# A two-layer decoder trunk: another timetable for the RWKV scan, with the Gram mask on GpSimd and the keys by per-channel constants

## The chip, the core and the metric

The kernel runs on one core of one Trainium2 chip. The metric is device time in microseconds (us) of one execution. The engines are TensorE (PE; its weight loads are shown as PEld), VectorE (DVE), ScalarE (ACT), GpSimd (POOL) and SyncE (SP, which only issues DMAs here). Each engine works through its own queue in order, and engines wait for each other by semaphores.

## The reference, cut to what matters

x is 512 x 2048 in float32. Layer 0 is gated differential attention, layer 1 is gated RWKV-7 time mixing. Each is `x + W_out(mixer(RMSNorm(x)) * silu(gate))`. All weights are float32. The second layer is:

```python
p = h @ w_in                                  # 2048 -> r, k, v, g of 2048 each, and two low ranks of 96
p = p + (token_shift(p) - p) * mu
decay = exp(-exp(w_log));  a = sigmoid(a0 + da @ iclr_up)
kk = k * k_k, normalised per head;  k = k * (1 + (a - 1) * k_a)
# per head (32 heads of 64), over 512 tokens:
sa = S @ (-kk_t);  S = S * w_t + sa (kk_t * a_t)' + v_t k_t';  y_t = S @ r_t
y = groupnorm(y) + sum(r * k * r_k) * v
out = x + (y * silu(g)) @ w_out
```

## The kernel before, in words

**Products.** Every float32 product with a weight is made of three float32r matmuls (`mm3`, L108): high times high, high times low, low times high. The weights arrive by DMA on SP (`load_w`, L78); ACT writes the high part (`split_w`, L96) and DVE the low part (L97), in two buffers each, so the split of one group can begin when PE is through with the group two before it. One group is 24 matmuls of 512 columns. These matmuls to the PSUM tile `pp` are called filler below, because the small work of the scan is laid between them.

**Layer 1** goes through 16 pairs of heads (`layer1`, loop over j). A round has four projections of 48 matmuls each: k, r and v of pair j and, from j = 3 (`LAG`), the gate of pair j-3. Beside them run:

- `stage1`: decay and learning rate; the cumulative sum of the log decay (`tensor_tensor_scan`, L731), its exponentials `E` and `l`; the tile `BK`, which holds for each head both the b vector and the key, each times `l` (L748, L751, L753, all on DVE); `AR` (a and r times `E`).
- `gram` (called after 15 of v's 48 matmuls, argument `behind`): BK' AR per chunk of 64 tokens into PSUM `gp` (L781), masked by the constant `gmask` on DVE into `p.G` (L788). The blocks that make a triangular system go out to DRAM (`ltd`, DMAs on POOL, L795 and L801) and come back as `LT` (L825).
- `t_solve`: 31 steps of two DVE instructions (L836, L838) on `LT` give `Tm`, which goes out as `td` (SP, L840).
- a chain of steps for the pair before (`chain`, `Chain`): `t_combine` loads `TT` (L852), transposes a part (`T1`, L860, DVE) and completes it with two sets of small matmuls, `px` (L866, L876). `scan_pair` then goes over 8 chunks. Each chunk has three small matmuls, each followed by a hand-over: `sm` L943, copied to `rhs` on ACT (L946); L954, copied to `VS` on ACT (L956); L961, from which DVE makes the next state in `VS` (L965, for the first chunk L968). POOL copies the state (`SA`, L949) and scales it (`Sg`, L952); L965 reads `Sg`, and the ACT copy L956 overwrites what L949 reads.
- `outputs` (PSUM `Y`, L983, L987), `centre`, `group_norm`, `finish_y` and, three rounds later, `gate`.

**What orders it.** `tick` counts filler matmuls. When a chain's count (`gap` after the two ACT hand-overs, `gap_s` after the state) is used up, its next step may be issued after that matmul (`issue_after`); a scheduler then places it in each engine's queue by a modelled time and a priority, of which the scan's (`SCAN`) stands over that of the weights (`AHEAD`). `Chain.held` adds a condition: a step that needs ACT or DVE (`taker`) waits while the position `at` in the projection lies in certain windows. In rounds 3 to 14 the gaps are 5 and 5 matmuls, else 4 and 4, and in the last chain 3 and 4.

**Between the layers** (`layer0`, L554 to L569) the row norms of the new x are needed before the first matmul of layer 1: sums of squares (`ssx`), `rsqrt` as a row of small DVE operations for three row tiles, then for the fourth, and x scaled by it (L566).

Of the kernel before, what the change touches and what calls it, by code (L numbers as in the profile page):

```python
# [23 lines left out]
P = 128  # L24
# [80 lines left out]

def mm3(nc, out, aH, aL, bH, bL, start, stop, g=None, at=0):
    for i, (a, b, s, e) in enumerate(((aH, bH, start, False), (aH, bL, False, False), (aL, bH, False, stop))):
        m = nc.tensor.matmul(out, a, b, start=s, stop=e)  # L108
        if g:
            tick(g, m, at + i)  # L110
    return m


class Chain:

    def __init__(self, g, steps, delay=0):
        self.steps, self.wait, self.taker = steps, delay, None  # L120
        g.chains.append(self)

    def step(self, g):
        with g.tc.high_priority(offset=SCAN):
            self.wait, self.taker = next(self.steps, (None, None))
        if self.wait is None:
            g.chains.remove(self)
# [12 lines left out]
def tick(g, m, at):  # L140
# [179 lines left out]
def attention(g, h, qkT, qkL, sq, V, VL, G, gap, rows=None):  # L320
# [64 lines left out]
    for i in range(NT + 3):  # L385
        if 0 < i <= NT:
            turn(i - 1)
        if i > 2:
            turn_y(i - 3)
        if i == NT + 2:  # L390
            break
        yield 8, None
        if 1 < i < NT + 2:
            weigh(i - 2)
        if i < NT:
            scores(i)
        yield gap - 8, None
    if rows is None:
# [34 lines left out]
def layer0(g, aps):  # L433
# [71 lines left out]
    with ExitStack() as cx:  # L505
# [3 lines left out]
        for h in range(NH):  # L509
# [5 lines left out]
            def keys(t1s=t1s, qkT=qkT):  # L515
                for t in range(NT):
                    turn_qk(g, t1s, *qkT, t)
                    yield 20, None

# [31 lines left out]

        rs = g.small.tile([P, NT], F32, name="rs1", tag="rs1", bufs=1)
        ss = g.small.tile([P, NT], F32, name="ss1", tag="ss1", bufs=1)
        for a, b in ((0, NT - 1), (NT - 1, NT)):  # L554
            nc.vector.reduce_sum(ss[:, a:b], g.ssx[:, a:b, :], AX.X)
            nc.vector.tensor_scalar(ss[:, a:b], ss[:, a:b], 1.0 / D, EPS, ALU.mult, ALU.add)
            rsqrt(g, rs[:, a:b], ss[:, a:b], b - a, f"r{b - a}")

        def more_h(n, m):
            for k in range(len(g.hH), min(n, KT)):  # L560
                xq, c0 = xs[k // 4], k % 4 * P
                ps = g.ps.tile([P, 512], F32, name="xT", tag="pa", bufs=2)
                for t in range(NT):
                    if c0 == 0:
                        with tc.high_priority(offset=AHEAD):
                            nc.vector.tensor_scalar(xq[:, t, :], xq[:, t, :], rs[:, t : t + 1], None, ALU.mult)  # L566
                    with tc.issue_after(m.ins) if m else ExitStack():
                        nc.tensor.transpose(ps[:, t * P : (t + 1) * P], xq[:, t, c0 : c0 + P], g.ident[:])
                with tc.high_priority(offset=AHEAD):  # L569
                    make_h(g, ps, KT + k)  # L570
# [33 lines left out]
def unit_chan(g, parts, cols, step=P, more=None, behind=(0, None)):  # L604
# [6 lines left out]
    for k0 in range(0, KT, KG):  # L611
        wh, wl = split_w(g, parts, KG, cols, k0)
        for k, c in [(k, c) for k in range(KG) for c in range(n)]:
            s = slice(c * step, (c + 1) * step)
            kk = k0 + k
            if more and c == 0:
                more(kk + 2, m)
            m = mm3(nc, pts[c][:step, :], wh[:, k, s], wl[:, k, s], g.hH[kk][:], g.hL[kk][:],
                    kk == 0, kk == KT - 1, g, 3 * kk)
            if n == 1 and 3 * kk + 3 == behind[0]:  # L620
# [14 lines left out]
C = 64  # L635
# [8 lines left out]
def rwkv_consts(g, aps):  # L644
# [17 lines left out]
    for nm, i, a, b in (("hw0", 0, 0.5, 0.0), ("ha0", 1, 0.5, 0.0), ("kk", 2, 1.0, 0.0), ("nkk", 2, -1.0, 0.0),  # L662
# [4 lines left out]
        g.prm[nm] = o  # L667


def rwkv_masks(g):  # L670
# [3 lines left out]
    nc.gpsimd.memset(g.rmask[:, :, 0:1], 0.0)  # L674
    g.TT = c.tile([P, NC_, 2, C], F32, name="TT")
    nc.gpsimd.memset(g.TT[:], 0.0)
    g.gmask = c.tile([P, P], BF16, name="gmask")
    nc.gpsimd.memset(g.gmask[:], 1.0)
    for lo in (0, C):
        r = slice(lo, lo + C)  # L680
        nc.gpsimd.affine_select(out=g.gmask[r, 0:C], in_=g.gmask[r, 0:C], compare_op=ALU.is_ge, fill=0.0,
                                base=-1, pattern=[[1, C]], channel_multiplier=-1)
        nc.gpsimd.affine_select(out=g.gmask[r, C:P], in_=g.gmask[r, C:P], compare_op=ALU.is_ge, fill=0.0,
                                base=0, pattern=[[1, C]], channel_multiplier=-1)
    g.hdec = c.tile([P, 1], F32, name="hdec")
# [28 lines left out]
def stage1(g, j, k, up):  # L714
# [32 lines left out]
    nc.scalar.activation(f[:], tha[:], AF.Identity, bias=col("omka"), scale=col("hka"))  # L747
    nc.vector.scalar_tensor_tensor(tha[:], tha[:], 1.0, k[:], ALU.add, ALU.mult)  # L748
    nc.vector.tensor_mul(f[:], f[:], k[:])
    for h, r_ in ((0, slice(0, C)), (1, slice(C, P))):  # L750
        nc.vector.scalar_tensor_tensor(BK[r_, :, h, :], ch(tha[r_, :]), col("hkk")[r_, :], l[r_, :, :],  # L751
                                       ALU.mult, ALU.mult)
        nc.vector.tensor_mul(BK[r_, :, 1 - h, :], ch(f[r_, :]), l[r_, :, :])  # L753
    k2 = w.tile([P, T], F32, name="k2", tag="thg", bufs=1)
# [15 lines left out]
def gram(g, j, p, before):  # L770
# [15 lines left out]
    for c0, gp in halves:  # L786
        for h in range(2):
            nc.vector.tensor_mul(p.G[:, c0 : c0 + 4, :, h, :], gp[h][:].rearrange("p (u x t) -> p u x t", u=4, x=2),  # L788
                                 g.gmask[:].rearrange("p (x t) -> p x t", x=2)[:, None].to_broadcast([P, 4, 2, C]))
    ps = g.ps.tile([P, 512], F32, name="pt", tag="pb", bufs=2)  # L790
# [55 lines left out]
def t_combine(g, j, p):  # L846

    nc, w, TT = g.nc, g.work, g.TT
    for h in range(2):
# [8 lines left out]
    for h in range(2):  # L858
        r_ = slice(h * C, h * C + C)
        nc.vector.transpose(T1[r_], TT[r_, :, h, 0:HALF])  # L860
    yield GAP_D, None
    N = NC_ * HALF
# [7 lines left out]
    for h, b0, _, _ in blocks:  # L870
        r_ = slice(b0, b0 + C)
        nc.scalar.copy(p.G[r_, :, 0, h, :], p.AR[r_, :, 0, :])
    yield GAP_X, None
    for h, b0, lo, hi in blocks:
# [3 lines left out]
    for h, b0, lo, _ in blocks:  # L878
        nc.scalar.copy(TT[lo, :, h, HALF:C], px[lo, N:].rearrange("p (c s) -> p c s", c=NC_))
    yield GAP_T, "ACT"  # L880

# [50 lines left out]
def scan_pair(g, j, p, gap, gap_s, others):  # L932
# [8 lines left out]
    for c in range(NC_):  # L941
# [8 lines left out]
        if 0 < c < NC_ - 1:  # L950
            Sg = w.tile([P, C], F32, name="Sg", tag="Sg", bufs=2)
            nc.gpsimd.tensor_scalar(Sg[:], p.SA[:, c - 1, :], p.gam[:, c : c + 1], None, ALU.mult)  # L952
        yield gap, "ACT"
        nc.tensor.matmul(sm[:, P : P + C], both(g.TT[:, c]), rhs[:], start=True, stop=True)  # L954
        for h, r_ in HEADS:
            nc.scalar.copy(VS[r_, c, h, :], sm[r_, P : P + C])  # L956
        yield (gap, "DVE") if c < NC_ - 1 else (gap, None)
        if c == NC_ - 1:
# [10 lines left out]
        if c in others:  # L969
            others[c]()  # L970
        yield gap_s, "ACT"
    outputs(g, j, p)
# [53 lines left out]
def layer1(g, aps):  # L1026
    nc, tc = g.nc, g.tc
    with ExitStack() as cx:
# [6 lines left out]
        for j in range(D // P):  # L1035
# [29 lines left out]

            vps = proj(2, behind=(15, behind))
            stage_v(g, j, p, vps)
# [11 lines left out]
        gps = [proj(3, i) for i in (j - 1, j)]  # L1079
        rows = split_rows(g, g.yd2, ("r", "k"), 2, j - 1)  # L1080
        rows.append(gate(g, j - 1, pairs[j - 1], gps[0], True))
# [4 lines left out]
        for cb in range(4):  # L1086
            cs = slice(cb * 512, (cb + 1) * 512)
            pts = unit_tok(g, yH, yL, [(aps["rw_w_out"][0], cb * 512, 512)], 512, 2)
            for t in range(NT):
                xr = w.tile([P, 512], F32, name="xr1", tag="rk"[t % 2], bufs=2)  # L1090
                nc.sync.dma_start(out=xr[:], in_=g.xd[t * P : (t + 1) * P, cs])
# [49 lines left out]
```

## Time and profile before

| what | us |
|---|---|
| runs before: median of 3 (lowest to highest) | 2263.07 (2261.76 to 2263.41) |
| profiled execution | 2254.08 |
| its span, first to last instruction | 2252.3 |
| PE busy in it | 2178.0 (97%) |
| DVE busy | 1422.2 (63%) |
| ACT busy | 955.2 (42%) |
| POOL busy | 228.8 (10%) |

A row of the grouped view gives line, engine, operation, tiles (output <- inputs), shape and count, then busy time and mean ns of one, then the idle time of the engine just ahead of them with what ended it. A row of the timeline gives start, duration, engine, line, tiles and, in brackets, the idle time ahead of it and its releaser. A row of the waits reads: waiting engine and line <- releaser: us in total, number of times, longest. Matmuls overlap in the pipeline and their ends are modelled: a 512-column matmul is shown with 0.39 us, while the next one starts 0.23 us after it.

### The profile page before, as it was taken

The numbers are of one execution on the slowest core, as the hardware profiler recorded it, in microseconds if no ns is written. First come the engines' busy times: TensorE is split into PE (matmuls) and PEld (weight loads), VectorE is DVE, ScalarE is ACT, GpSimd is POOL, SyncE is SP. The second block draws the span as 40 slices with busy tenths as digits, with TensorE's granted clock in tenths as the row PEclk, the third lists the DMA queues.
The fourth block names the chain that finished last, engine by engine and source line by source line (L and its number), as shares of the span: only waits on it lengthen the run. The fifth ranks groups of instructions, "written<-read, shape, count | busy, mean of one in ns | idle before, by whom it ended". The sixth has DMA issues, their size and how long they took to land. (4 is left out here: it accounts for less than half of the span.)

```text
span 2252.3 us, 33774 instructions
## 1 busy us (share of the span) xinstructions
PE 2178.0 (97%) x12260; PEld 1770.4 (79%) x12260; DVE 1422.2 (63%) x3783; ACT 955.2 (42%) x1969; POOL 228.8 (10%) x612
## 2 busy tenths in 40 slices
PE   8999999999999999989999999999999999999999
PEld 6888888888888878867767777777777777777887
DVE  5555646465564673346778887777777888776322
ACT  5443434344343452224355545545454455545211
POOL 0000000000000000000222212222222222222000
PEclk9999999999999999989999999999999999999999
DMA  6222232222322263323423233333333333334433
GB/s 179 93 86 95 84 100 88 93 94 82 97 85 94 94 214 108 136 77 87 105 66 77 78 87 95 87 90 89 85 89 80 89 88 90 96 97 127 140 131 112
DMA packets 290729, 224.45 MB, mean 100 GB/s; under 512 B 47732, under 2 KB 255748, under 8 KB 290564
## 3 DMA queue, kind: packets, MB, share of 16 engines
q1 hardware_dynamic: 275892, 195.74, 29.3%
q0 software_dynamic: 6144, 10.84, 2.0%
q10 hardware_dynamic: 8528, 15.73, 1.8%
q8 instruction: 96, 1.57, 0.3%
q14 instruction: 69, 0.57, 0.1%
HBM read 202.26 MB, written 19.99 MB: 99 GB/s over the span
## 5 line engine op out<-in xcount | busy, mean ns | idle before, releaser
L97 DVE TENSOR_TENSOR wl<-wraw,wh 128x1024 fp32r<-128x1024 f32 (+2 forms) x325 | 396.0, 1219 | 541.2 <-ACT wh L96 534.6
L96 ACT CAST wh<-wraw 128x1024 fp32r<-128x1024 f32 (+2 forms) x325 | 339.9, 1046 | 595.0 <-PE pp L108 404.1
L108 PE MATMUL pp<-wh,hH 128*128 128x512 f32 x1408 | 554.4, 394 | 6.0 <-ACT hH L588 5.7
L108 PE MATMUL pp<-wh,hL 128*128 128x512 f32 x1408 | 552.3, 393 | 0.0
L108 PE MATMUL pp<-wl,hH 128*128 128x512 f32 x1408 | 552.2, 392 | 0.0
L108 PE MATMUL pp<-hH,wh 128*128 128x512 f32 (+1 forms) x1056 | 429.3, 407 | 2.3 <-DVE mixt L631 1.7
L108 PE MATMUL pp<-hL,wh 128*128 128x512 f32 (+1 forms) x1056 | 428.5, 406 | 0.1
L108 PE MATMUL pp<-hH,wl 128*128 128x512 f32 (+1 forms) x1056 | 423.7, 401 | 0.0
L108 PEld LDWEIGHTS pp<-wh,hH 128*128 128x128 f32 x1408 | 265.0, 188 | 60.4 <-ACT hH L588 6.4
L108 PEld LDWEIGHTS pp<-wh,hL 128*128 128x128 f32 x1408 | 265.0, 188 | 53.6 <-DVE hL L589 0.3
L108 PEld LDWEIGHTS pp<-wl,hH 128*128 128x128 f32 x1408 | 265.2, 188 | 52.5
L108 PEld LDWEIGHTS pp<-hH,wh 128*128 128x128 f32 (+1 forms) x1056 | 198.7, 188 | 39.0 <-DVE mixt L631 2.2
L108 PEld LDWEIGHTS pp<-hH,wl 128*128 128x128 f32 (+1 forms) x1056 | 198.9, 188 | 36.7 <-issue 1.5
L108 PEld LDWEIGHTS pp<-hL,wh 128*128 128x128 f32 (+1 forms) x1056 | 199.2, 189 | 35.1 <-DVE hL L589 1.5
L836 DVE SCALAR_TENSOR_TENSOR tmpl<-LT,Tm 128x60 f32<-128x60 f32 (+24 forms) x496 | 133.9, 270 | 12.2
L946 ACT COPY rhs<-sm 64x64 f32<-64x64 f32 x256 | 52.9, 206 | 158.5 <-PE sm L943 154.5
L838 DVE TENSOR_TENSOR Tm<-Tm,tmpl 128x60 f32<-128x60 f32 (+24 forms) x496 | 104.8, 211 | 12.7
L949 POOL COPY SA<-VS 64x64 f32<-64x64 f32 x224 | 60.1, 268 | 476.2 <-DVE VS L965 390.6
L943 PEld LDWEIGHTS sm<-VS,G 128*128 128x128 f32 x256 | 41.6, 188 | 64.8 <-PE pp L108 48.8
L943 PE MATMUL sm<-VS,G 128*128 128x128 f32 x256 | 55.2, 297 | 32.6 <-DVE VS L965 27.0
L673 POOL MEMSET rmask<- 128x512 bf16 x1 | 0.5, 527 | 833.0 <-DVE nb L340 833.0
L956 ACT COPY VS<-sm 64x64 f32<-64x64 f32 x256 | 52.8, 206 | 59.0 <-PE sm L954 51.5
(262 smaller groups left out, 2745.0 us busy)
## 6 DMA issues: line engine op xcount, KB each, us to landing
wraw<-in_rw_w_in_dram SPq DMA_DIRECT2D x128, 512.0 KB, 3.8
wraw<-in_da_w_in_dram SPq DMA_DIRECT2D x254, 256.0 KB, 3.0
wraw<-in_da_w_out_dram SPq DMA_DIRECT2D x32, 512.0 KB, 3.6
wraw<-in_rw_w_out_dram SPq DMA_DIRECT2D x32, 512.0 KB, 3.7
LT<-ltd POOLq DMA_DIRECT2D x64, 132.0 KB, 2.9
yr<-yd SPq DMA_DIRECT2D x28, 256.0 KB, 3.9
xq<-in_x_dram SPq DMA_DIRECT2D x16, 256.0 KB, 4.7
xd<-xq ACTq DMA_DIRECT2D x16, 256.0 KB, 3.3
```

Source lines behind the costliest of these rows:

```text
L96: nc.scalar.copy(hi[:, ks], raw[:, ks])
L97: nc.vector.tensor_sub(lo[:, ks], raw[:, ks], hi[:, ks].bitcast(F32))
L108: m = nc.tensor.matmul(out, a, b, start=s, stop=e)
L673: nc.gpsimd.memset(g.rmask[:], 1.0)
L836: nc.vector.scalar_tensor_tensor(tt, LT[:, i : i + 1, i + 1 :].to_broadcast([P, s, n]), n2[:, i : i + 1], Tm[:, 0:s, i : i + 1].to_broadca ...
L838: nc.vector.tensor_add(Tm[:, 0:s, i + 1 :], Tm[:, 0:s, i + 1 :], tt)
L943: nc.tensor.matmul(sm[:, 0:P], both(p.G[:, c, 0]), both(VS[:, c]), start=True, stop=True)
L946: nc.scalar.copy(rhs[r_, :], sm[r_, h * C : h * C + C])
L949: nc.gpsimd.tensor_copy(p.SA[r_, c - 1, :], VS[r_, c, h, :])
L956: nc.scalar.copy(VS[r_, c, h, :], sm[r_, P : P + C])
```

## The change

- **Timetable of the scan.** `held` and the windows are gone. Chains have gaps of 6 (ACT hand-overs) and 8 (states) in rounds 3 to 14, and 4 and 5 in the other rounds. A pair's chain is finished not at the start of the next chain but in `behind`, ahead of `gram`, which is called after 18 of v's matmuls. The transposes of keys, values and y sit at chunks 0, 1, 2 and 3 where they were at 3, 4, 2 and 5.
- **T doubled.** `TT` is two tiles used by turns; `AR` has three buffers, `k` and `r` have one each, and the tiles that load rows at the end take four tags with one buffer each.
- **Gram.** ACT copies `gp` to `p.G` (4 copies in a round) where DVE multiplied by the mask. After the blocks for the triangular system have been sent, POOL zeroes what must be zero with four `affine_select` instructions (two over 64 x 512, two over 64 x 1024 elements) ahead of the loads of `LT` in its queue.
- **Keys.** Instead of one product on DVE and four half-width ones, ACT makes both factors of `BK` by a per-channel scale and bias (two `activation`, constants `bk_s`, `bk_b` made once), and DVE makes k times `l` and one product over 128 x 1024.
- **Between the layers.** The norm is computed for all four row tiles at once with the priority `SOLVE`, and the scaling of x has no priority of its own.

```diff
-    def held(self, at):
-        if self.taker == "ACT":
-            return not (9 <= at <= 21 or 27 <= at <= 43)
-        return self.taker == "DVE" and (1 <= at < 12 or 26 <= at < 32)
...
-        if c.wait <= 0 and not c.held(at):
+        if c.wait <= 0:
...
-        for a, b in ((0, NT - 1), (NT - 1, NT)):
-            nc.vector.reduce_sum(ss[:, a:b], g.ssx[:, a:b, :], AX.X)
-            nc.vector.tensor_scalar(ss[:, a:b], ss[:, a:b], 1.0 / D, EPS, ALU.mult, ALU.add)
-            rsqrt(g, rs[:, a:b], ss[:, a:b], b - a, f"r{b - a}")
+        with tc.high_priority(offset=SOLVE):
+            nc.vector.reduce_sum(ss[:], g.ssx[:], AX.X)
+            nc.vector.tensor_scalar(ss[:], ss[:], 1.0 / D, EPS, ALU.mult, ALU.add)
+            rsqrt(g, rs[:], ss[:], NT, "r4")
...
-                        with tc.high_priority(offset=AHEAD):
-                            nc.vector.tensor_scalar(xq[:, t, :], xq[:, t, :], rs[:, t : t + 1], None, ALU.mult)
+                        nc.vector.tensor_scalar(xq[:, t, :], xq[:, t, :], rs[:, t : t + 1], None, ALU.mult)
...
+    g.TT = [c.tile([P, NC_, 2, C], F32, name=f"TT{i}") for i in range(2)]
...
-    p.AR = w.tile([P, NC_, 2, C], F32, name="AR", tag="AR", bufs=2)
+    p.AR = w.tile([P, NC_, 2, C], F32, name="AR", tag="AR", bufs=3)
...
-    nc.vector.scalar_tensor_tensor(tha[:], tha[:], 1.0, k[:], ALU.add, ALU.mult)
+    for i in range(2):
+        nc.scalar.activation(BK[:, :, i, :], ch(tha[:]), AF.Identity, bias=col(f"bk_b{i}"), scale=col(f"bk_s{i}"))
     nc.vector.tensor_mul(f[:], f[:], k[:])
-    for h, r_ in ((0, slice(0, C)), (1, slice(C, P))):
-        nc.vector.scalar_tensor_tensor(BK[r_, :, h, :], ch(tha[r_, :]), col("hkk")[r_, :], l[r_, :, :],
-                                       ALU.mult, ALU.mult)
-        nc.vector.tensor_mul(BK[r_, :, 1 - h, :], ch(f[r_, :]), l[r_, :, :])
+    nc.vector.tensor_mul(l[:], ch(k[:]), l[:])
+    nc.vector.tensor_mul(BK[:], BK[:], l[:, :, None, :].to_broadcast([P, NC_, 2, C]))
...
-            nc.vector.tensor_mul(p.G[:, c0 : c0 + 4, :, h, :], gp[h][:].rearrange("p (u x t) -> p u x t", u=4, x=2),
-                                 g.gmask[:].rearrange("p (x t) -> p x t", x=2)[:, None].to_broadcast([P, 4, 2, C]))
+            nc.scalar.copy(p.G[:, c0 : c0 + 4, :, h, :], gp[h][:].rearrange("p (u x t) -> p u x t", u=4, x=2))
...
+    for h in range(2):
+        r_ = slice(h * C, h * C + C)
+        nc.gpsimd.affine_select(out=p.G[r_, :, 0, 1 - h, :], in_=p.G[r_, :, 0, 1 - h, :], compare_op=ALU.is_ge,
+                                fill=0.0, base=-1, pattern=[[0, NC_], [1, C]], channel_multiplier=-1)
+        nc.gpsimd.affine_select(out=p.G[r_, :, 1], in_=p.G[r_, :, 1], compare_op=ALU.is_ge, fill=0.0, base=0,
+                                pattern=[[0, NC_], [0, 2], [1, C]], channel_multiplier=-1)
...
-            p = stage1(g, j, shift_mix(g, proj(1), P, *mus(g, 1, j), "k"), up)
-            r = shift_mix(g, proj(0), P, *mus(g, 0, j), "r")
+            p = stage1(g, j, shift_mix(g, proj(1), P, *mus(g, 1, j), "k", 1), up)
+            r = shift_mix(g, proj(0), P, *mus(g, 0, j), "r", 1)
...
+                others = [(0, lambda p=p: turn_keys(g, p, 0)), (1, lambda p=p: turn_keys(g, p, 4)),
+                          (2, lambda p=p: turn_values(g, p))]
+                if j > 1:
+                    others.append((3, lambda i=j - 2: finish_y(g, i, pairs[i])))
+                full = LAG <= j < D // P - 1
+                chain(g, j - 1, pairs[j - 1], 5, 6 if full else 4, 8 if full else 5, others).step(g)
+            stage2(g, j, r, p)
+
+            def behind(m, j=j, p=p):
                 if j > 1:
                     pairs[j - 2].chain.finish(g)
-                others = [(2, lambda p=p: turn_values(g, p)), (3, lambda p=p: turn_keys(g, p, 0)),
-                          (4, lambda p=p: turn_keys(g, p, 4))]
-                if j > 1:
-                    others.append((5, lambda i=j - 2: finish_y(g, i, pairs[i])))
-                full = LAG <= j < D // P - 1
-                chain(g, j - 1, pairs[j - 1], 5, 5 if full else 4, 5 if full else 4, others).step(g)
-            stage2(g, j, r, p)
-
-            def behind(m, j=j, p=p):
                 with tc.issue_after(m.ins):
                     gram(g, j, p, j and pairs[j - 1].chain)
...
-            vps = proj(2, behind=(15, behind))
+            vps = proj(2, behind=(18, behind))
```

More of the change, by code (lines that the diff above doesn't have):

```diff
@@ L119, in __init__ @@
     def __init__(self, g, steps, delay=0):
-        self.steps, self.wait, self.taker = steps, delay, None
+        self.steps, self.wait = steps, delay
         g.chains.append(self)
@@ L124, in step @@
         with g.tc.high_priority(offset=SCAN):
-            self.wait, self.taker = next(self.steps, (None, None))
+            self.wait = next(self.steps, None)
         if self.wait is None:
@@ L667, in rwkv_consts @@
         g.prm[nm] = o
+    for nm, first, second in (("bk_s0", "hkk", "hka"), ("bk_b0", "hkk", "omka"),
+                              ("bk_s1", "hka", "hkk"), ("bk_b1", "omka", "hkk")):
+        o = c.tile([P, 16], F32, name="prm_" + nm)
+        nc.vector.tensor_copy(o[:C], g.prm[first][:C])
+        nc.vector.tensor_copy(o[C:], g.prm[second][C:])
+        g.prm[nm] = o
 def rwkv_masks(g):
@@ L674, in rwkv_masks @@
     nc.gpsimd.memset(g.rmask[:, :, 0:1], 0.0)
[L675 to L684, printed above, removed]
+    g.TT = [c.tile([P, NC_, 2, C], F32, name=f"TT{i}") for i in range(2)]
+    for TT in g.TT:
+        nc.gpsimd.memset(TT[:], 0.0)
     g.hdec = c.tile([P, 1], F32, name="hdec")
@@ L952, in scan_pair @@
             nc.gpsimd.tensor_scalar(Sg[:], p.SA[:, c - 1, :], p.gam[:, c : c + 1], None, ALU.mult)
-        yield gap, "ACT"
-        nc.tensor.matmul(sm[:, P : P + C], both(g.TT[:, c]), rhs[:], start=True, stop=True)
+        yield gap
+        nc.tensor.matmul(sm[:, P : P + C], both(g.TT[j % 2][:, c]), rhs[:], start=True, stop=True)
         for h, r_ in HEADS:
             nc.scalar.copy(VS[r_, c, h, :], sm[r_, P : P + C])
-        yield (gap, "DVE") if c < NC_ - 1 else (gap, None)
+        yield gap
         if c == NC_ - 1:
```

34 lines of the change are left out of this document (17 added, 17 removed).

## The prediction

> **What bounds the kernel now.** I read the page's first part, then PE's waits, then the timeline of one steady round of layer 1 and of the border between the layers, then durations grouped by form.
>
> ```profile
> span 2252.3 us, 33774 instructions
> PE 2178.0 (97%) x12260; PEld 1770.4 (79%) x12260; DVE 1422.2 (63%) x3783; ACT 955.2 (42%) x1969; POOL 228.8 (10%) x612
> ```
> ```profile
> PE sm L943 <- DVE VS L965: 27.0, 40, 1.3
> PE xT L568 <- DVE xq L566: 9.4, 2, 5.0
> PE sm L943 <- DVE VS L968: 5.2, 6, 1.6
> PE px L866 <- DVE T L860: 4.1, 3, 3.1
> PE sm L961 <- ACT VS L956: 0.2, 1, 0.2
> ```
>
> PE is the bound, and the change leaves its instructions alone: only its waits can go or come. Of these 32.2 us (46 times) end with the state that DVE makes, 9.4 us are at the border, and next to nothing waits for ACT. The shown idle is a little short, because matmul ends are modelled:
>
> ```profile
> 1403.73 0.40 PE L108 MATMUL pp<-hH,wl 128*128 128x512 f32 x1
> 1404.63 0.46 PE L943 MATMUL sm<-VS,G 128*128 128x128 f32 x2 [0.51 <-DVE VS L965]
> ...
> 1453.43 0.46 PE L943 MATMUL sm<-VS,G 128*128 128x128 f32 x2 [0.72 <-DVE VS L965]
> ...
> 1462.86 0.46 PE L943 MATMUL sm<-VS,G 128*128 128x128 f32 x2 [0.95 <-DVE VS L965]
> ...
> 1468.67 0.46 PE L943 MATMUL sm<-VS,G 128*128 128x128 f32 x2 [0.51 <-DVE VS L965]
> ```
>
> Filler matmuls start 0.23 apart (the front text says so); here 0.90 passes, so 0.67 is lost where 0.51 is shown: 0.16 more each time. The prize at the states is 32.2 + 46 x 0.16 = 39.6 us. The last three rows are one round's: 0.72 + 0.95 + 0.51 + 3 x 0.16 = 2.7 us, with the share of L968 about 3.0.
>
> **The border: a gain of 3.9 us.** Ends of the queues at the border:
>
> ```profile
> 994.03 0.39 PE L108 MATMUL pp<-wh,hL 128*128 128x512 f32 x1
> ...
> 1005.46 0.69 PE L568 MATMUL xT<-ident,xq 128*128 128x128 f32 x2 [4.39 <-DVE xq L566]
> 1006.71 1.17 PE L108 MATMUL pp<-hH,wh 128*96 128x512 f32 x2 [0.56 <-ACT hH L588]
> ```
> ```profile
> 996.38 0.19 ACT L550 ACTIVATION_READ_ACCUMULATOR junkx<-xq 128x1 f32 x1
> ```
> ```profile
> 998.61 0.16 DVE L70 SCALAR_TENSOR_TENSOR rs<-rs_t,rs_i 128x3 f32<-128x3 f32 x1
> 998.80 4.84 DVE L566 TENSOR_SCALAR xq<-xq,rs 128x512 f32<-128x512 f32 x12
> ```
>
> The last sum of squares is there at 996.6. Before, DVE scales twelve tiles (4.84 us, 0.40 each) ahead of the fourth norm, and the first product starts at 1006.7. In the built order of the changed program the 13 small operations come first, by the spacing of 0.2 us until 999.2; four scalings (1.6) end at 1000.8, four transposes at about 1001.8 (a little slow after idling), `hH` takes 0.7, `hL` stands behind eight scalings (1002.4) and takes 0.75: products run from 1002.8. Gain 3.9; bounds 0 (if the order of DVE's later scalings starves the next `hL`) and 5.5 (fourth norm at once).
>
> **Work that moves.** Durations by form:
>
> ```profile
> L97 DVE TENSOR_TENSOR wl<-wraw,wh 128x1024 fp32r<-128x1024 f32 x319 | 390.8, 1225 | 528.2 <-ACT wh L96 521.6 <-DMA xr<-xd 4.2 <-PE pp L108 2.0
> L96 ACT CAST wh<-wraw 128x1024 fp32r<-128x1024 f32 x319 | 335.3, 1051 | 587.9 <-PE pp L108 397.9 <-PE pt L108 120.7 <-issue 55.9
> L788 DVE TENSOR_TENSOR G<-gp,gmask 128x512 f32<-128x512 f32 x64 | 40.2, 684 | 3.5 <-PE gp L781 3.5
> L751 DVE SCALAR_TENSOR_TENSOR BK<-th,prm_hkk,l 64x512 f32<-64x512 f32 x32 | 23.8, 745 | 0.9 <-ACT l L739 0.4
> L753 DVE TENSOR_TENSOR BK<-f,l 64x512 f32<-64x512 f32 x32 | 21.9, 683 | 0.2
> L748 DVE SCALAR_TENSOR_TENSOR th<-th,mixk 128x512 f32<-128x512 f32 x16 | 11.0, 684 | 0.0
> L812 ACT COPY BKT<-pt 128x512 f32<-128x512 f32 x32 | 18.7, 587 | 36.2 <-PE pt L811 18.2 <-DVE tmpl L836 16.4 <-DVE Tm L838 1.5
> L872 ACT COPY G<-AR 64x512 f32<-64x512 f32 x32 | 19.8, 618 | 59.9 <-PE px L866 59.3
> L869 ACT COPY X<-px 32x256 f32<-32x256 f32 x32 | 11.7, 364 | 4.9 <-PE px L866 4.5
> L747 ACT ACTIVATE f<-th,prm_omka,prm_hka 128x512 f32<-128x512 f32 x16 | 13.1, 818 | 0.0
> L503 POOL TENSOR_SCALAR_AFFINE_SELECT mask<-mask 128x512 f32<-128x512 f32 x1 | 0.6, 611 | 0.0
> ```
>
> Per round DVE loses 4 masks (2.74), L748 (0.68), 2 x 0.745 and 2 x 0.683, and gains k times `l` (0.68, as L788) and one product over 1024 (1.23, as L97): 6.28 less 1.91, 4.4 us lighter. ACT gains 4 copies (2.35) and 2 activations (1.64): 4.0 us heavier. POOL gains two selects of 0.61 and two that I put at 1.04 (a straight line up to twice the size): 3.3 us. None is PE time; what counts is who stands ahead of a hand-over. The two `TT` let the load go out as soon as `td` is there; before, it came late by the old scan and was hidden all the same. Single `k` and `r` cost nothing: their readers end half a round before the next write.
>
> **The states: DVE waits shrink.** The shortest hand-overs I find:
>
> ```profile
> 1152.58 0.49 PE L961 MATMUL sm<-VS,BKT 128*128 128x128 f32 x2
> ...
> 1154.12 0.46 PE L943 MATMUL sm<-VS,G 128*128 128x128 f32 x2
> ...
> 1155.09 0.43 PE L954 MATMUL sm<-rhs,TT 128*128 128x64 f32 x2
> ...
> 1156.11 0.49 PE L961 MATMUL sm<-VS,BKT 128*128 128x128 f32 x2
> ```
>
> A state takes 1.54, a hand-over to ACT 0.97 or 1.02. With n fillers between, PE comes round after 0.22 + 0.23 n: 1.37 for n = 5, 2.06 for n = 8, 1.60 for n = 6. So a state had no slack and gets 0.5 us; an ACT step gets 0.6. I walked one changed round along the built queues with these durations. Chunks 0 to 5 find DVE in time (one is 0.1 late). Chunk 6 does not: the split of r's second group can start only when k's last matmul is done, and behind it on DVE stand the mix of k, the cumulative sum (1.22) and four more of 0.68 before the state; it is ready 8.8 us after k's end, while PE stands there after 7.5. Left: 1.35 + 0.1 = 1.45 of the 3.0 per round.
>
> **The ACT hand-overs: new waits.** With `held` gone, four are late. The largest is in chunk 0, just behind the Gram:
>
> ```profile
> 1414.01 2.06 PE L781 MATMUL gp<-AR,BK 64*128 64x128 f32 x32
> 1416.00 1.09 PE L866 MATMUL px<-T,G 32*32 32x32 f32 x32
> 1417.02 0.40 PE L710 MATMUL pt<-sHx,ones 128*2 128x512 f32 x1
> ```
>
> In the built order PE does px, Gram, px with nothing between (1.0 + 2.0 + 1.0), two `ones` and 8 fillers: L943 at 6.5 us, L954 due at 8.1. ACT begins at 0.7 and has ahead of `rhs`: two copies of 0.62, X (0.73), a small cast (0.35), four Gram copies (2.35), T (0.73), two of 512 columns (1.17), a weight cast (1.05): free at 8.3, `rhs` done 8.7, L954 at 8.95. Late by 0.9. The other three: chunk 2's L954 behind a weight cast (0.3), chunk 2's L961, which has only one filler and two transposes in front (0.45), chunk 6's L961 behind two activations on decay and rate (0.3). Sum 1.95 per round, where there was none. Bounds: 0 (none shown before) and 16 x 0.5 = 8 (each behind half a weight cast).
>
> **Sum.** Twelve steady rounds: 1.45 + 1.95 - 3.0 = +0.4 each. Before each Gram PE also lost about 0.3 us waiting for `AR`; three fillers later it is there. Net 0.1 x 12 = +1. In round 1 `T` is late: the built order puts px 27 fillers (6.2 us) sooner, and DVE is 4.4 lighter, so the wait of 3.1 grows by 1.8, and the lighter DVE saves most of the other two waits for `T` (1.0): +1. The rounds 1 and 2 get one filler more at each state (5 for 4); of their waits, in the stretch from 1000 to 1250 us, only two can use it:
>
> ```profile
> PE sm L943 <- DVE VS L965: 1.1, 2, 0.9
> ```
>
> that is -0.5. The rest is as before: -3.9 + 1 + 1 - 0.5 = -2.4, with the single terms good to some 3 us. On the profiled 2254.1 us that is 2251.7; the profile is 9.0 under the median, so I forecast 2260 (0.13% less than before).
>
> **Rivals.**
>
> *The wide gaps work and ACT is in time.* The waits for ACT do not appear: 12 x 1.95 = 23 less, 2237. For it: in before ACT already waits at `rhs` for PE, so the scheduler puts scan copies early. Against: `rhs` of chunk 0 is behind 2.35 us of new copies.
>
> *ACT is the new bottleneck of the scan (slower).* Place: the 16 hand-overs per round. If each is late 0.12 us more than walked, that is 1.9 per round, 23 in all: 2283. It decides against the change when ACT's waits pass 2.15 us per round (1.95 + 2.4/12); slower by what can be measured (4.5 us more) from 2.5. For it: 4.0 us more work on ACT, no windows.
>
> *POOL is late.* The four selects stand ahead of `LT` and of the copy L949 that L956 of chunk 1 must wait for:
>
> ```profile
> L825 POOL DMA_DIRECT2D LT<-ltd x64 | 31.7, 502 | 59.0 <-DMA ltd<-ssl 46.0 <-DMA ltd<-G 7.1 <-DVE Tm L839 3.6
> ```
>
> POOL idles 46.0/16 = 2.9 us per round there for its own DMAs, which covers the 3.3 almost; I find 3 us of slack more at chunk 1. It decides from 6.4 us for the four; at 8 us it costs 1.6 x 12 = 19: 2279.
>
> ```profile
> 1441.79 1.27 DVE L97 TENSOR_TENSOR wl<-wraw,wh 128x1024 fp32r<-128x1024 f32 x1
> ```
> ```profile
> 1442.07 1.29 POOL L952 TENSOR_SCALAR Sg<-SA,gam 128x64 f32<-128x64 f32 x1
> ```
>
> POOL's 0.44 us scaling takes 1.29 while such a weight difference runs. The Trainium skill (SBUF — State Buffer, Who interferes with whom) says that a DVE operation with two SBUF inputs and a GpSimd read exclude each other for a whole instruction; this pair agrees. By that rule each select could wait out one L97, 4 x 1.23 more, and this rival would come true; in the built DVE queue only one L97 stands in that stretch.
>
> **Chances.** Forecast 0.45 (own range 2250 to 2268), ACT in time 0.20, ACT late 0.28, POOL late 0.07. 0.2% is 4.5 us, about what a measurement of this kernel can tell from no change. The bound for faster, 2258.5, cuts the forecast's case near its middle. Faster: 0.20 + 0.20 of the forecast's 0.45 = 0.40; same 0.20; slower 0.28 + 0.07 + 0.05 = 0.40. The range, 2234 to 2285, takes in both sides' cases.
>
> **What would show it.** Right: the wait at the first L943 state of chunks 1 to 5 nearly gone, one of about 1.2 us left at chunk 6 or 7; new PE waits for `rhs` and `VS` from ACT, some 25 to 30 us in all; the first product of layer 1 four us sooner after the last of layer 0; selects near 0.6 and 1.0 us. Wrong: PE waits for ACT below 10 us or above 45, or px waiting for `T` in the steady rounds, which would mean that the chain from Gram to `T` has become longer than a round (I find 2.6 us of slack).

## The result and the profile after

The changed kernel takes 2247.8 us (median of 4 runs, 2247.2 to 2250.5), the kernel before 2263.2 beside it: a ratio of 0.9935, with a 95% interval of 0.9917 to 0.9952. In a later comparison both were measured again: 2247.3 and 2259.2, ratio 0.9954 (0.9939 to 0.9969). The change makes the kernel 10 to 15 us faster. The forecast, 2260 us, had the sign and too little of the size; 2248 lies inside the range, between the forecast and the rival "the wide gaps work and ACT is in time" (2237).

The first part of the page of after, and PE's waits:

```profile
span 2246.1 us, 33754 instructions
PE 2185.2 (97%) x12260; PEld 1767.5 (79%) x12260; DVE 1382.1 (62%) x3666; ACT 1006.9 (45%) x2065; POOL 285.5 (13%) x672
```
```profile
PE sm L941 <- DVE VS L963: 14.8, 14, 1.2
PE px L864 <- DVE T L858: 6.4, 3, 4.4
...
PE xT L561 <- DVE xq L559: 5.4, 1, 5.4
...
PE sm L941 <- DVE VS L966: 2.9, 1, 2.9
PE sm L952 <- ACT rhs L944: 1.4, 3, 0.8
PE sm L959 <- ACT VS L954: 1.2, 4, 0.4
```

The state waits fell from 32.2 us (46 times) to 17.7 (15 times): one is left in nearly every steady round, 1.2 us at the last chunk. The waits for ACT that I feared are 2.6 us in all. T is waited for longer, 6.4 us for 4.1.

A steady round can be read from the place of `px` in successive rounds, before and after:

```profile
1734.34 1.09 PE L866 MATMUL px<-T,G 32*32 32x32 f32 x32
1797.82 1.09 PE L866 MATMUL px<-T,G 32*32 32x32 f32 x32
```
```profile
1728.25 1.09 PE L864 MATMUL px<-T,G 32*32 32x32 f32 x32
1790.96 1.09 PE L864 MATMUL px<-T,G 32*32 32x32 f32 x32
```

63.48 us became 62.71. For the whole of layer 1 I counted the fillers on PE (96 for the low ranks, 144 in each of the rounds 0 to 2, 192 in each later one, then three gates of 48) and took the time between the first fillers of neighbouring stretches. The profiled executions differ so (us, after less before; the sums are taken before rounding):

| stretch | predicted | measured | second profiles |
|---|---|---|---|
| border | -3.9 | -4.5 (12.68 to 8.20) | -4.5 |
| low ranks behind it | 0 | -1.1 | -0.2 |
| rounds 0 to 3 (T of the first pairs, states) | +0.5 | +3.9 (rounds 2 and 3) | -0.5 |
| rounds 4 to 14 | +1 (said of 3 to 14) | -2.6: nine rounds at 62.77 for 63.52, round 4 +0.6, round 10 +3.5 | -4.2 |
| round 15 and the last gates | 0 | -2.2 | -2.1 |
| layer 0, the last product | 0 | +0.5 (+0.6 and -0.2) | -2.6 |
| sum | -2.4 | -6.2 (spans: 2252.3 to 2246.1) | -14.0 (2258.8 to 2244.7) |

The last column compares a second profiled execution of each kernel, which the experiments below describe. The two columns agree at the border and in the last rounds. They differ where the granted clock fell in one execution and not in another, so a difference of a few us in one row isn't yet the change's.

### The profile page after: what moved, and what is told of

Same layout as the page of the kernel before. It is cut to its first block, busy times and chain, and to the rows that moved or that the text cites. A ratio compares the mean times of both kernels' runs of the same rounds, so it can differ in the third digit from the quotient of the medians.

```text
span 2246.1 us, 33754 instructions
## 1 busy us (share of the span) xinstructions
PE 2185.2 (97%) x12260; PEld 1767.5 (79%) x12260; DVE 1382.1 (62%) x3666; ACT 1006.9 (45%) x2065; POOL 285.5 (13%) x672
## 5 line engine op out<-in xcount | busy, mean ns | idle before, releaser
L108 PE MATMUL pp<-hH,wl 128*128 128x512 f32 (+1 forms) x1056 | 428.8, 406 | 0.0
L963 DVE SCALAR_TENSOR_TENSOR VS<-sm,gam,Sg 64x64 f32<-64x64 f32 x192 | 54.3, 283 | 52.7 <-PE sm L959 48.6
L944 ACT COPY rhs<-sm 64x64 f32<-64x64 f32 x256 | 52.5, 205 | 72.8 <-PE sm L941 70.1
L941 PEld LDWEIGHTS sm<-VS,G 128*128 128x128 f32 x256 | 43.4, 188 | 43.1 <-issue 29.5
```

What stands on the lines that cost most here:

```text
L941: nc.tensor.matmul(sm[:, 0:P], both(p.G[:, c, 0]), both(VS[:, c]), start=True, stop=True)
L944: nc.scalar.copy(rhs[r_, :], sm[r_, h * C : h * C + C])
L963: nc.vector.scalar_tensor_tensor(VS[r_, c + 1, h, :], s_, p.gam[r_, c : c + 1], Sg[r_, :], ALU.mult, ALU.add)
```

## The experiments

Two theories for the steady rounds. A: the wide gaps find the states ready, and the work moved off DVE is worth little. B: the lighter DVE is what counts. Ratios are to the kernel before, measured beside each run; the changed kernel stands at 0.9954 on the same scale. "Mean round" is that of nine steady rounds (5 to 9, 11 to 14): 63.52 before, 62.77 after.

**The kernel before once more** (no edit).

> The unchanged kernel before, profiled once more. The first profile of it (2254.1 us) is 9 us under its median (2263). If that execution was a lucky one, this one takes 2261 to 2265 us and its trace shows where 9 us more are lost; if the two levels belong to the chip, it is the same within 0.2% as the runs beside it and its waits are those of the first profile (state waits about 32 us).

2259.7 us, ratio 1.0001 (0.9991 to 1.0011). The waits are those of the first profile (state waits 27.3 and 4.5), the mean round is 63.49, and yet the span is 2258.8 us, 6.5 longer. What differs is the granted clock behind the same waits, that for T above all. First profile, then this one (stretch, its length, busy time of PE, PEld, DVE, ACT and POOL, the granted clock, DMA share, GB/s):

```profile
1127.62 0.77 PE L866 MATMUL px<-T,G 32*32 32x32 f32 x16 [3.13 <-DVE T L860]
```
```profile
1130.00:1140.00 10.00, 10.00 (x85) 7.40 (x85) 5.91 (x22) 5.58 (x15) 0.94 (x3) 0.93 0.18 50
```
```profile
1129.93 1.05 PE L866 MATMUL px<-T,G 32*32 32x32 f32 x16 [3.46 <-DVE T L860]
```
```profile
1130.00:1140.00 10.00, 10.00 (x78) 7.54 (x79) 4.70 (x16) 2.98 (x8) 0.00 (x0) 0.50 0.19 52
```

Round 2 takes 62.2 us in the one and 66.7 in the other. Followed in the clock records of the traces, the clock behind this wait is 0.50 for 3.41 us in the first profile (1128.07 to 1131.48) and for 13.65 us here (1129.19 to 1142.84). Layer 0 ends 2.5 us later too: behind a wait of 1.94 us at 815 us the clock is 0.50 for 6.83 us, where the first profile has a wait of 1.82 us at the same place and no lower clock behind it. Summed over the execution in windows of 10 us, (1 - clock) x 10 us gives a loss of 10.2 us in the first profile and 17.6 here: 7.4 more, where the span is 6.5 longer. The first profile was an execution with little loss, not a constant 9 us away from the runs.

**Only the gaps, in the kernel before.**

```diff
     def held(self, at):
-        if self.taker == "ACT":
-            return not (9 <= at <= 21 or 27 <= at <= 43)
-        return self.taker == "DVE" and (1 <= at < 12 or 26 <= at < 32)
+        return False
...
-                chain(g, j - 1, pairs[j - 1], 5, 5 if full else 4, 5 if full else 4, others).step(g)
+                chain(g, j - 1, pairs[j - 1], 5, 6 if full else 4, 8 if full else 5, others).step(g)
```

> The kernel before with only the windows taken out and the gaps at 6 and 8 matmuls (4 and 5 in the other rounds). Mask and keys stay on DVE, T is single, the border is as before. Theory A (the wide gaps find the states ready, the moved work is worth little): state waits fall from 32 us to 15 to 20, time 8 to 12 us under before, about 2253. Theory B (the lighter DVE is what counts): state waits stay near 30 us, time within 3 us of before.

2258.7 us, ratio 1.0002 (0.9991 to 1.0013). The state waits go, as A said, but others come:

```profile
PE sm L959 <- ACT VS L954: 14.1, 18, 1.0
...
PE sm L941 <- DVE VS L963: 6.4, 14, 0.8
```

The mean round is 63.17, 0.32 less than in the profile just shown. Round 2 takes 71.4 us (66.7 in the profile beside it), round 15 and the gates 4.8 more, and both hold windows of low clock (0.67 and 0.69). But this profiled execution was the longest of ten, 8.5 us over their median, so where the median execution loses the gain of the steady rounds is not shown. By the ratio the gaps alone gain nothing.

**Only the gaps taken back, in the changed kernel.**

```diff
-                chain(g, j - 1, pairs[j - 1], 5, 6 if full else 4, 8 if full else 5, others).step(g)
+                chain(g, j - 1, pairs[j - 1], 5, 5 if full else 4, 5 if full else 5, others).step(g)
```

> The changed kernel with gaps of 5 and 5 where it has 6 and 8 (4 and 5 elsewhere as it has). Theory A: a state takes 1.54 us and PE is back after 1.37, so six states a round lose 0.17 us or more and chunk 6 still waits: 12 to 30 us over the changed kernel, 2260 to 2278. Theory B: the lighter DVE carries the gain, time within 4 us of the changed kernel (2248).

2253.8 us, ratio 0.9979 (0.9969 to 0.9989): less than A said, more than B.

```profile
PE sm L941 <- DVE VS L963: 14.5, 24, 1.0
PE sm L952 <- ACT rhs L944: 9.9, 26, 1.7
```

The mean round is 63.16; round 3 is 5 us longer than in the changed kernel (77.9 for 72.8), with the clock at 0.59 in one window. So the gaps alone and the rest of the change alone each bring about 0.35 us a round, and both together 0.75. Theory A doesn't stand by itself. Whether the rest is theory B's lighter DVE is asked by the runs with the mask and with the keys back on DVE.

**More room at the last state.**

```diff
-        yield gap_s
+        yield gap_s + 6 if c == NC_ - 2 and gap_s == 8 else gap_s
```

> The changed kernel with 14 matmuls in place of 8 behind the state of the last scan step in rounds 3 to 14, where its trace still shows a wait of 1.2 us in each round. Theory A (DVE is late by a fixed 1.3 us there, at the end of k): the wait goes, 12 x 1.2 = 14 us less, 2234. Rival: the scheduler puts other DVE work ahead of the state again, and the time stays at 2248 within 3 us.

2250.7 us, ratio 0.9958 (0.9943 to 0.9974): no gain, the rival was right, though by another engine. DVE's state is in time now; the next hand-over is late by nearly the same (waits for `rhs` are 16.8 us in all, 1.4 in the changed kernel):

```profile
1906.31 0.44 PE L941 MATMUL sm<-VS,G 128*128 128x128 f32 x2
...
1909.27 0.43 PE L952 MATMUL sm<-rhs,TT 128*128 128x64 f32 x2 [1.14 <-ACT rhs L944]
```
```profile
1907.12 1.04 ACT L96 CAST wh<-wraw 128x1024 fp32r<-128x1024 f32 x1
...
1908.16 0.60 ACT L592 CAST sHx<-k 128x512 fp32r<-128x512 f32 x1
1908.79 0.42 ACT L944 COPY rhs<-sm 64x64 f32<-64x64 f32 x2
```

In the changed kernel the copy to `rhs` goes ahead of this weight cast. With the state due later, the scheduler puts the cast and `sHx` first.

**The changed kernel once more** (no edit).

> The unchanged changed kernel on this chip, beside the kernel before. If the gain is the kernels' own, the ratio is that of the first comparison, 0.9917 to 0.9952, some 2243 to 2250 us where the kernel before takes 2259. The trace shows the wait at the last state (1.2 us in each steady round) again, and the stretches of low granted clock at the same places but with other depths (10 us of loss in its first profile, 10 and 18 in the two of the kernel before).

2247.3 us, ratio 0.9954. Mean round 62.76, state waits 14.9 us (14 times), border 8.20, loss by the clock 7.9 us.

**PE kept busy at the border.**

```diff
+        warm = g.ps.tile([P, 512], F32, name="xT", tag="pa", bufs=2)
+        with tc.issue_after(g.m.ins):
+            for i in range(22):
+                nc.tensor.matmul(warm[:], yH[KT - 1][:, 0:P], yH[KT - 1][:], start=True, stop=True)
```

> The changed kernel with 22 matmuls of 512 columns more, whose product is not used, on PE between the last product of layer 0 and the transposes of layer 1, where PE waits 5.4 us for the norm. If idle time is what lowers the granted clock, the border stays at 8.2 us but the clock between 1000 and 1010 us is granted at 1.0 where it was 0.66 to 0.72, and the 96 matmuls behind the border take 30 to 31 us in place of 32.2 to 32.7: 1.5 to 3 us less. If the clock drops there for another reason, no change.

The trace shows what was expected of the clock, after first and this kernel second:

```profile
1000.00:1010.00 10.00, 9.19 (x40) 6.36 (x41) 8.97 (x20) 2.70 (x5) 0.00 (x0) 0.72 0.00 0
```
```profile
1000.00:1010.00 10.00, 8.82 (x46) 5.96 (x46) 9.58 (x21) 3.42 (x6) 0.00 (x0) 1.00 0.01 2
```

The low ranks take 31.1 us where they took 32.2 and 32.5. So it is the idle time that lowers the clock here. The time, 2249.0 us (ratio 0.9955), doesn't show it: in this execution the clock fell deeper behind the waits for T (0.59 for 0.95 between 1230 and 1240 us), and the gain of 1.2 us is under what the runs spread.

**The mask back on DVE.** The constant `gmask`, made once as before, and the smaller buffers are left out here.

```diff
-            nc.scalar.copy(p.G[:, c0 : c0 + 4, :, h, :], gp[h][:].rearrange("p (u x t) -> p u x t", u=4, x=2))
+            nc.vector.tensor_mul(p.G[:, c0 : c0 + 4, :, h, :], gp[h][:].rearrange("p (u x t) -> p u x t", u=4, x=2),
+                                 g.gmask[:].rearrange("p (x t) -> p x t", x=2)[:, None].to_broadcast([P, 4, 2, C]))
...
-        nc.gpsimd.affine_select(out=p.G[r_, :, 0, 1 - h, :], in_=p.G[r_, :, 0, 1 - h, :], compare_op=ALU.is_ge,
-                                fill=0.0, base=-1, pattern=[[0, NC_], [1, C]], channel_multiplier=-1)
-        nc.gpsimd.affine_select(out=p.G[r_, :, 1], in_=p.G[r_, :, 1], compare_op=ALU.is_ge, fill=0.0, base=0,
-                                pattern=[[0, NC_], [0, 2], [1, C]], channel_multiplier=-1)
```

> The changed kernel with the Gram mask back on DVE (four products with the constant, no copies on ACT, no selects on POOL; two small tiles have two buffers for three to make room). Theory A (ACT's row of copies behind the Gram is what makes the first step 0.3 us late, and DVE has idle time there): that wait goes, 12 x 0.3 = 4 us less than the changed kernel, and no state wait comes back. Theory B (mask off DVE is part of the gain): 4 to 10 us more, with state waits.

2235.0 us, ratio 0.9896 (0.9880 to 0.9913): 12 us under the changed kernel. A had the sign and a third of the size. The mean round is 62.24 (0.5 less), although the last state is now later:

```profile
PE sm L943 <- DVE VS L965: 18.2, 12, 1.6
```

Rounds 2 and 3 take 6 us less together (131.2 for 137.3 in the changed kernel's second profile). There the scheduler puts the first `px` behind 305 fillers of the rounds and not behind 291, so PE waits less, and the clock stays at 1.0 between 1110 and 1240 us. After first, then this kernel:

```profile
1117.95 0.82 PE L864 MATMUL px<-T,G 32*32 32x32 f32 x16 [4.44 <-DVE T L858]
```
```profile
1119.18 0.69 PE L866 MATMUL px<-T,G 32*32 32x32 f32 x16 [1.92 <-DVE T L860]
```

**The selects alone taken away**, with the copies left on ACT.

```diff
-            nc.scalar.copy(p.G[:, c0 : c0 + 4, :, h, :], gp[h][:].rearrange("p (u x t) -> p u x t", u=4, x=2))
+            nc.scalar.activation(p.G[:, c0 : c0 + 4, :, h, :], gp[h][:].rearrange("p (u x t) -> p u x t", u=4, x=2),
+                                 AF.Copy, scale=0.0)
...
-        nc.gpsimd.affine_select(...)
-        nc.gpsimd.affine_select(...)
```

> The changed kernel without the four selects on POOL; the Gram copies stay on ACT, but scale by zero, so that what is not masked stays finite: masking and the products with the Gram are left out of what is computed, the instructions beside the selects stay. With the mask on DVE the changed kernel took 2235 us for 2247. Theory A (ACT's row of copies and the place of the T products in PE's queue make the 12 us): within 3 us of 2247. Theory B (the selects, 3.6 us on POOL ahead of the T loads and of the state copies, make them): 2235 to 2238.

2245.4 us, ratio 0.9928 (0.9913 to 0.9943), about halfway between the two. The mean round is 62.25, the same as with the mask on DVE: in the steady rounds, taking away the selects alone gains as much as moving the whole mask back, 0.5 us a round. `px` stands behind 291 fillers as in the changed kernel, and rounds 2 and 3 stay long (64.0 and 75.0). By the traces the other half of the 12 us belongs to the place of `px` and to the clock behind its wait; no run moves `px` alone.

**The keys back on DVE.**

```diff
-    for i in range(2):
-        nc.scalar.activation(BK[:, :, i, :], ch(tha[:]), AF.Identity, bias=col(f"bk_b{i}"), scale=col(f"bk_s{i}"))
+    nc.vector.scalar_tensor_tensor(tha[:], tha[:], 1.0, k[:], ALU.add, ALU.mult)
     nc.vector.tensor_mul(f[:], f[:], k[:])
-    nc.vector.tensor_mul(l[:], ch(k[:]), l[:])
-    nc.vector.tensor_mul(BK[:], BK[:], l[:, :, None, :].to_broadcast([P, NC_, 2, C]))
+    for h, r_ in ((0, slice(0, C)), (1, slice(C, P))):
+        nc.vector.scalar_tensor_tensor(BK[r_, :, h, :], ch(tha[r_, :]), col("hkk")[r_, :], l[r_, :, :],
+                                       ALU.mult, ALU.mult)
+        nc.vector.tensor_mul(BK[r_, :, 1 - h, :], ch(f[r_, :]), l[r_, :, :])
```

> The changed kernel with the keys made on DVE as before (five products there, none on ACT): DVE 1.9 us a round heavier in the stretch behind k, ACT 1.6 lighter. Theory A (the keys stand behind the late state in DVE's queue): within 3 us of the changed kernel. Theory B (the lighter DVE behind k is what keeps the last state at 1.2 us): the wait there grows by up to 1.9 us, 10 to 20 us more.

2251.8 us, ratio 0.9966 (0.9953 to 0.9979). The mean round is 62.77 and the state wait 14.7 us, both as in the changed kernel: that is A, the keys stand behind the late state, though the time is 4.5 us more by the medians (2.7 by the ratios) where A allowed 3. The difference lies at the start and in the clock: T is waited for 8.0 us for 6.2, and the loss by the clock is 13.1 us for 7.9.

The two runs speak against theory B: neither the mask nor the keys, put back on DVE alone, makes a steady round longer. Both at once were not tried. What the rest of the change brings beside the gaps, 0.36 us a round, would then lie in the other hunks (two tiles for T, the order of the transposes, the Gram three fillers later, the end of the chain), and no run takes these apart.

**Twice the copies on ACT.**

```diff
             nc.scalar.copy(p.G[:, c0 : c0 + 4, :, h, :], gp[h][:].rearrange("p (u x t) -> p u x t", u=4, x=2))
+            nc.scalar.copy(p.G[:, c0 : c0 + 4, :, h, :], gp[h][:].rearrange("p (u x t) -> p u x t", u=4, x=2))
```

> The changed kernel with each of the four Gram copies on ACT issued twice, 2.06 us a round more on ACT behind the Gram. Theory A (ACT has no slack there, the first step is already 0.33 us late): the wait grows to about 2.3 us in every steady round, 12 x 2 = 24 us more, 2271. Rival (the scheduler lets other work of ACT stand back): less than 5 us more.

2271.0 us, ratio 1.0049 (1.0029 to 1.0069): by the ratios 0.95% or 21 us over the changed kernel, where A said 24. The cost is not the one wait of 2.3 us that A named but several:

```profile
PE sm L953 <- ACT rhs L945: 13.4, 26, 1.9
PE sm L942 <- DVE VS L964: 10.0, 20, 1.1
PE pt L703 <- ACT G L781: 6.5, 15, 0.8
```

The mean round is 64.57, 1.8 longer for 2.06 us of copies. ACT has no room behind the Gram. Two more microseconds of work there are enough to make the kernel slower than the one before, which is what the rival "ACT late" said.

**The border alone, in the kernel before** (its two hunks of the change's diff).

> The kernel before with the border of the changed one alone (one norm for four row tiles, the scaling without a priority). Theory: border 12.7 to 8.2 us, and the low ranks behind it, where the granted clock recovers, 0.5 to 1 us shorter: 5 us under the kernel before, 2253 to 2255. Rival (what comes earlier there is waited for at T of the first pair): no change.

2256.8 us, ratio 0.9980 (0.9970 to 0.9991), 4.5 us less by the ratio, as the theory said. The border is 8.19 us long. So a third to nearly a half of the change's 10 to 15 us comes from the border.

**The mask on DVE and room at both of the last hand-overs.** To the edit with the mask on DVE comes:

```diff
-        yield gap
+        yield gap + 5 if c == NC_ - 1 and gap_s == 8 else gap
         nc.tensor.matmul(sm[:, P : P + C], both(g.TT[j % 2][:, c]), rhs[:], start=True, stop=True)
...
-        yield gap_s
+        yield gap_s + 6 if c == NC_ - 2 and gap_s == 8 else gap_s
```

> The changed kernel with the mask on DVE, and with 14 matmuls for 8 behind the state of the last step and 11 for 6 behind the product that follows it, in rounds 3 to 14. Theory A (the wait of 1.5 us there is DVE's lateness at the end of k, and both hand-overs behind it have room now): 12 x 1.5 = 18 us less than with the mask on DVE alone, 2217. Theory B (as with 14 matmuls alone, the scheduler lets the hand-over stand back and the wait comes back at the next step): 2233 to 2237.

2221.5 us, ratio 0.9823 (0.9808 to 0.9838). By the ratios that is 0.73% or 16 us under the mask on DVE alone; A said 18. The steady waits are gone, the mean round is 61.07:

```profile
PE px L866 <- DVE T L860: 3.0, 3, 2.0
PE sm L943 <- DVE VS L968: 2.4, 2, 2.2
...
PE sm L961 <- ACT VS L956: 1.5, 3, 0.6
...
PE sm L954 <- ACT rhs L946: 1.2, 2, 0.8
```

It is the fastest of all kernels here, by the ratios 1.3% or 30 us under the changed one.

## Why the prediction was right, and where its sum was off

The time lies in the range and the kernel became faster, as forecast. But the direction was little better than a coin toss by the prediction's own chances (faster 0.40, slower 0.40), and the steady round, forecast 0.1 us longer, became 0.75 us shorter. So the terms have to be looked at one by one.

**The border: right.** Products of layer 1 were to begin 3.9 us sooner. After:

```profile
994.67 0.39 PE L108 MATMUL pp<-wh,hL 128*128 128x512 f32 x1
1000.46 2.06 PE L561 MATMUL xT<-ident,xq 128*128 128x128 f32 x8 [5.40 <-DVE xq L559]
1002.87 1.17 PE L108 MATMUL pp<-hH,wh 128*96 128x512 f32 x2 [0.35 <-ACT hH L581]
```

They begin 1002.87 - 994.67 = 8.20 us behind layer 0, where it was 12.68: 4.5. The start of 1002.8 was met; layer 0 had ended 0.6 later. What I left out is the low ranks behind it (-1.1, and -0.2 in the second profiles): the shorter idle time leaves the clock higher, 0.72 for 0.50 between 1000 and 1010 us.

**The states: right.** Chunks 0 to 5 were to find DVE in time, and 1.35 us were to be left at the last state; shown are 1.2 us, and by the spacing it is 1.34. The reason is the one given, work that waits for the end of k, though the queue differs from the one I walked: two operations of 0.68 stand there and not four, and small steps of T's solve, at the dots, fill the rest.

```profile
1837.45 1.22 DVE L724 TENSOR_TENSOR_SCAN l<-rmask,th 128x512 f32<-128x512 bf16 x1
...
1838.79 0.68 DVE L743 TENSOR_TENSOR f<-f,mixk 128x512 f32<-128x512 f32 x1
...
1839.49 0.68 DVE L729 TENSOR_TENSOR l<-l,m 128x512 f32<-128x512 f32 x1
...
1840.62 0.29 DVE L963 SCALAR_TENSOR_TENSOR VS<-sm,gam,Sg 64x64 f32<-64x64 f32 x1
```
```profile
1841.06 0.46 PE L941 MATMUL sm<-VS,G 128*128 128x128 f32 x2 [1.20 <-DVE VS L963]
```

**The hand-overs to ACT: the step that was mis-sized.** I had 1.95 us a round, some 25 to 30 us of shown waits in all, and called less than 10 us a sign of being wrong. Shown are 2.6 us, so by its own sign this part of the mechanism failed: nearly all of the hand-overs to ACT are in time. In chunk 0 I had 0.9:

```profile
1790.96 1.09 PE L864 MATMUL px<-T,G 32*32 32x32 f32 x32
...
1797.31 0.39 PE L941 MATMUL sm<-VS,G 128*128 128x128 f32 x2
1799.24 0.43 PE L952 MATMUL sm<-rhs,TT 128*128 128x64 f32 x2
```
```profile
1791.68 0.62 ACT L870 COPY G<-AR 64x512 f32<-64x512 f32 x1 [3.15 <-PE px L864]
...
1794.14 2.06 ACT L780 COPY G<-gp 128x512 f32<-128x512 f32 x4
...
1798.78 0.41 ACT L944 COPY rhs<-sm 64x64 f32<-64x64 f32 x2
```

From L941 to L952 pass 1.93 us, where this kernel's other chunks with six fillers take 1.61: 0.32 late. The queue is the one I walked, but I added single durations: the four copies take 2.06 us in a row, not 4 x 0.59 = 2.35, because each begins before the one ahead has ended (they start 0.48 apart). The row from the first copy to the end of `rhs` is 7.5 us and not 8.0. Of the other three, chunk 2's L959 shows about 0.3 us, and the two others nothing. Together some 0.7 for 1.95. With 0.7 the steady sum would have been 1.45 + 0.7 - 3.0 - 0.3 = -1.15 a round; measured is -0.75, and the next paragraph names a cost of the size that lies between.

**POOL: a cost that the rival had and the sum had not.** The selects took a little more than was assumed (0.61 and 1.04):

```profile
L800 POOL TENSOR_SCALAR_AFFINE_SELECT G<-G 64x1024 f32<-64x1024 f32 x32 | 38.1, 1190 | 0.1
...
L798 POOL TENSOR_SCALAR_AFFINE_SELECT G<-G 64x512 f32<-64x512 f32 x32 | 21.4, 669 | 1.6
```

That is 3.7 us a round. Most of it falls into the time in which POOL would wait for its own DMAs: the loads of `LT` begin 11.6 us behind the first product of the Gram in most steady rounds, and 10.6 without the selects. No PE wait names POOL, and still the selects cost 0.5 us a round, as the run without them shows. With them L959 of chunk 1 is placed behind 11 fillers and not 7, and the last gap of chunk 2 shrinks from six fillers to one and two transposes, where the 0.3 us just named is lost. That this goes by the state copies behind the selects in POOL's queue is my reading of the order, not shown by a run: these copies do end 1.3 us later, but ACT writes `VS` only 3.3 us after them. The rule of the Trainium skill (SBUF — State Buffer, Who interferes with whom) did not matter: 31 of the 32 large selects took 1.15 to 1.18 us. The one that ran beside a weight difference on DVE took 2.18, which agrees with it.

**T of the first pairs: the wait right, its worth not settled.** I said +1. The wait grew from 3.13 to 4.44 as forecast (+1.3 for +1.8), and the other waits did not vanish (1.9 us for 1.0). Rounds 2 and 3 lost 3.8 us against the first profile of before, but they gained 0.5 in the second profiles: the first profile's round 2 was a short one, with only 3.41 us of low clock behind its wait.

**The step from profile to median: wrong.** I took the profile's distance of 9.0 us from the median as fixed and added it. The changed kernel's profile is at its median (2247.9 and 2247.8), and before's second profile had 7.4 us more loss by the clock with the same waits. Without those 9 us the same sum gives 2251.7, which would have been 4 us off; in this reckoning three quarters of the miss come from here. That 2251.7 would have been so near is partly luck, for it starts from an execution of before with little loss. Between the second profiles, which lie 14.0 us apart, the sum of -2.4 misses by 11.6. Of this, 5.2 us are in rounds 4 to 14, 2.6 in layer 0 and the last product, and 2.1 in round 15 and the gates, for which no run shows the reason. No term stood for a difference in granted clock between the two kernels. Over the single runs, (1 - clock) x span is about 14 us before (46 runs) and 9 after (8 runs).

Of the rivals, "ACT in time" describes the waits best, though its 2237 us lies nearly as far from 2248 as the forecast does. "ACT late" was two microseconds of ACT work a round away, as the doubled copies show.

## What to carry to other kernels

Work moved off a busy engine is paid for where it lands, in an in-order queue: the mask on ACT and POOL gave back about 12 us, and the keys on ACT changed nothing in a steady round. The gain came from the border and, in the steady rounds, in like parts from the new gaps and from hunks that the runs do not take apart. A wait shown on one engine may be only the first of a chain of hand-overs: giving room to one moved it to the next, giving room to both took it away (1.5 us of wait, 1.2 us of each round). Add up a queue by the starts of a row of instructions, not by their durations, and compare two profiled executions only after the granted clock of each has been read stretch by stretch.

## What the runs showed of the hardware

A wait of PE of 3 to 5 us is followed by a stretch at half the clock whose length is not the same from run to run: 3.41 us behind a wait of 3.13, 13.65 us behind one of 3.46, with 4.5 us of difference in the same round. The Trainium skill (TensorE: Matmul & The Clock Gate, Part 1) tells of a free-running activity window of about 3.4 us and of a start-up that varies with its phase; a spread of that kind is what these two lengths show, and that the filling matmuls held the clock at 1.00 agrees with it. Waits of 1.4 to 1.9 us before `px` in round 3 were followed by 0.95 to 0.51 as well, which is shorter than one such window, while a wait of 1.7 to 1.8 us just behind the low ranks was followed by no lower clock in any trace. What decides it among these short waits stays open.

In every profile of both kernels POOL pauses 2.1 or 2.3 us at one DMA issue of round 10. In the changed kernel it falls between the two DMAs of `ssl`, whose buffer ACT needs next, and grows on its way to PE:

```profile
1670.79 0.58 POOL L786 DMA_DIRECT2D ltd<-ssl  x1 [2.31 <-issue]
```
```profile
1674.71 0.63 ACT L1006 ACTIVATE ysq<-yc 128x512 f32<-128x512 f32 x1 [4.36 <-DMA ltd<-ssl]
```
```profile
1676.71 0.46 PE L941 MATMUL sm<-VS,G 128*128 128x128 f32 x2 [2.88 <-DVE VS L966]
```

Round 10 takes 67.1 us there, 63.6 before, and 65.5 in the changed kernel's second profile. There the wait was 2.6 us and the clock stayed at 1.00, where it was 0.50 for 3.41 us behind the wait of 2.88. What the pause is stays open.
